# First rows as single transfers, two squares as operands by themselves, unread products beside the chain, and a bank cleared earlier, in a streaming encoder layer

## The chip, the cores and the metric

The kernel runs on one core of one Trainium2 chip. A core has TensorE (PE, the matrix products), VectorE (DVE), ScalarE (ACT), GpSimd (POOL) and SyncE (SP, here a queue that issues transfers); ACT also issues a few. Transfers run on 16 DMA engines. The metric is the device time of one execution in microseconds; a lower one is better. A change of less than 0.2% (about 4.5 us here) can hardly be told from none.

## The reference

One layer of a hybrid encoder over 2048 prompt tokens and 64 sample tokens, width 1024, in float32:

```
mod = silu(c) @ w_ada + b_ada          -> sh1, sc1, gt1, sh2, sc2, gt2
h   = rmsnorm(x, g1) * (1 + sc1) + sh1
u, q, k, v, o, gates = split(h @ w_in)
x   = x + gt1 * (concat(pool_mixer(u), mlstm(q, k, v, gates) * sigmoid(o)) @ w_out)
h2  = rmsnorm(x, g2) * (1 + sc2) + sh2
a, g = split(causal_conv3(h2 @ w_up) + b_conv)
x   = x + gt2 * ((silu(g) * a) @ w_down)
y   = rmsnorm(x, g_final)
```

rmsnorm(x, g) is x * rsqrt(mean(x*x) + 1e-6) * g. Beside y, the states of the pooling mixer, the matrix memory and the convolution are returned. Two places matter here: the first rmsnorm, with its modulation, of the first 512 tokens, and the last rmsnorm of the last 256 tokens.

## The kernel before, in words

Activations are kept with the 1024 features on partitions, as eight rows `x[k]` of 128 partitions, and tokens along the free dimension. Float32 products are made in three passes of a rounded format (`PASSES`): a weight or activation is split into a rounded part and a remainder. Small products stay in plain float32; each of these is two instructions on PE.

The attention part goes over four groups of 512 tokens (the last has the 64 samples besides), the feed-forward part over three groups of 704. In the last part of the last feed-forward group the down projection runs for two sections of columns, 0 to 448 and 448 to 704 (`ENDS`), so that the final norm of the first section runs beside the products of the second.

The order: SP's transfers and most of the attention part are placed by a planner, from estimated times and from the order in the text. Inside `tc.manual_schedule` the order on PE, ACT, DVE and POOL is that of the text; this holds for the first stage `first()` with the first V projection, and for the whole feed-forward part. Each engine works through its own queue in order.

Eight banks of 512 columns take PE's results: four of a pool `large` (`mm_ps()`), two of `small` and two of `third`; `m2_ps()` takes turns, two of `small` and then two of `third`.

The first stage. The first eight rows `x0` come as four transfers of two rows (L135, on SP's and ACT's queue by turns), then the small vectors `V` (L136). `first()` squares each row on ACT (L984), and DVE adds six of the squares into two accumulators (L989). Beside each row PE makes a product that nothing reads (L991, into `ptq`). `silu()` makes CA from V. `rstd_cols` (L485 to L493) sums the two accumulators over partitions by products with one column of ones, four blocks of tokens times two accumulators (L489), scales the sums on DVE and takes the power -0.5 on POOL. `mod_q(0)` makes the first quarter of the modulation: eight steps of four products with `CA` (L923), a copy by ACT (L930), a transposition (L932), and two additions on DVE into `MOD` (L936). Between its steps and its transposition stand four products (L1001) that spread the four columns of inverse roots over all partitions into `pr`. Then DVE scales the first rows by `pr` (L1005), PE makes two more unread products (L1010, into `psq`), `h0(0)` makes the normalised rows on ACT (L953), and the V projection starts (L1028).

The squares lie in the pool `scr` of five buffers. Two small operations that need `V` stand after the first stage in the text (L1420, L1421) and outside the written order.

The end. `down` makes a row's products (L1807), `down_end` adds them into the residual row on DVE (L1823), squares it on ACT and adds the square on POOL, except that the last row's square stays an operand of its own (L1833). `final_end` for the second section clears a bank on DVE (L1702), sums the squares over partitions (L1705), lets DVE work off some rows of the first section (`late[0]`, L1746), scales (L1661), takes the power on POOL (L1663), spreads the result twice (L1721), multiplies six rows on DVE (L1746) and two on POOL (L1759), and stores them (L1740).

Of the kernel before, what the change touches and what calls it, by code (L numbers as in the profile page):

```python
# [9 lines left out]
F32 = mybir.dt.float32  # L10
# [24 lines left out]
NH = 4  # L35
# [21 lines left out]
def tile_layer(ctx: ExitStack, tc: tile.TileContext, xT, vecs, cst, rst, w_mod, w_ada, w_qkou, w_v, w_pool,  # L57
# [75 lines left out]
    V = cp.tile([P, NV], F32, tag="V", name="V")  # L133
    for k in range(0, KD, 2):
        (act if k % 4 else nc.sync).dma_start(out=pair_of(x0[k:k + 2]), in_=xT[k:k + 2, :, 0:GT].rearrange("k p t -> p k t"))  # L135
    nc.sync.dma_start(out=V, in_=vecs)  # L136
# [675 lines left out]
    if True:  # L812
# [161 lines left out]
        def first():  # L974
# [4 lines left out]
            def silu():  # L979
                act.activation(CA.rearrange("p k s -> p s k"),  # L980
                               V[:, V_CP:V_CP + 16].rearrange("p (s k) -> p s k", s=2), AF.Silu)
            for k in range(KD):
                x, sq = x0[k], scr()
                act.activation(sq[:, :GT], x, AF.Square)  # L984
                if k < 2:
                    sums.append(sq)
                else:
                    acc = sums[k % 2]
                    dve.tensor_tensor(out=acc[:, :GT], in0=acc[:, :GT], in1=sq[:, :GT], op=ALU.add)  # L989

                pe.matmul(ptq[:, :256], x[:, :P], x[:, :256], start=True, stop=True)  # L991
            silu()
            rs = sm.tile([P, 5], F32, tag="rs", name="rs")
            rstd_cols(sums, o0, rs)
            mod = mod_q(0)
            for _ in range(KD + 1):
                next(mod)

            pr = third.tile([P, 512], F32, tag="bank", name="pr")
            for ti in range(4):  # L1000
                pe.matmul(pr[:, ti * P:(ti + 1) * P], rs[:, ti:ti + 1].broadcast_to([P, P]), ident, start=True, stop=True)  # L1001
            for _ in mod:
# [6 lines left out]
            for _ in range(2):  # L1009
                pe.matmul(psq[:, :256], x0[7][:, :P], x0[7][:, :256], start=True, stop=True)  # L1010
            us = h0(0)
# [392 lines left out]
        for o in groups:  # L1404
# [5 lines left out]
            if o.g == 0:  # L1410
                with tc.manual_schedule(engines={ET.PE, ET.Activation, ET.DVE, ET.Pool}):
                    ps_v = first()
                    small_inputs()
                    cols = []
                    va = proj_v(o, h, cols)
            else:
                cols = []
                va = proj_v(o, h, cols)
            if o.g == 0:
                dve.tensor_copy(M[:, GT + 1:GT + 2], RV[:, 2:3])  # L1420
                dve.tensor_scalar(out=GH, in0=V[:, V_GH:V_GH + NH], scalar1=0.5, scalar2=None, op0=ALU.mult)  # L1421
                t = scr()
# [264 lines left out]

    late, YLATE = [], 6

    def final_end(o, x3, sums, lo, hi):  # L1690
# [3 lines left out]
        for _ in range(4 if lo == 0 else 0):  # L1694
            yield
        ps = m2_ps()
        rs = f2.tile([P, 5], F32, tag="rs", name="rs", bufs=2)
        order = [(ti, i) for ti in range(len(tiles)) for i in range(len(sums))]
        if lo > 0:
            order.sort(key=lambda c: c[1])  # L1700
        if lo > 0:
            dve.memset(ps[:, :len(tiles)], 0.0)  # L1702
        for ti, i in order:
# [4 lines left out]
        if lo > 0:  # L1708
            late[0](YLATE)
        stat_cols(ps, rs, [n for (t, n) in tiles])  # L1710
        if lo > 0:
# [64 lines left out]
    for o in fgroups:  # L1776
        Bo = B[o.g]
        for pi, (f0, f1_) in enumerate(PARTS):
# [39 lines left out]
            def down_end(n, ps, secs):  # L1818
# [8 lines left out]
                lo, hi = secs[0][0], secs[-1][1]  # L1827
                if ends and n == KD - 1:
                    sq7 = fscr()
                    for (a, b, s) in o.segs:  # L1830
# [33 lines left out]
            for secs in [(c,) for c in ENDS] if ends else (both,):  # L1864
                sums = [(ssum, 0)]
                for n in range(NE, KD):
                    ps = [mm_ps() for _ in secs]
                    down(ps, rows[n], range(nf), secs, ends)
                    down_end(n, ps, secs)
# [89 lines left out]
```

## Time and profile before

| what | us |
|---|---|
| median of 3 runs | 2227.15 (2225.89 to 2227.29) |
| the profiled execution | 2230.81 |
| its span, first to last instruction | 2229.0 |
| PE busy, of the span | 2208.9 (99%) |
| DVE busy | 1572.2 (71%) |
| ACT busy | 1000.4 (45%) |

The 1.8 us between the profiled execution's time and its span lie around the span. A row of a timeline gives the start, the length, the engine, the line of the kernel, the operation, result and operands, the shape and how many instructions are merged; in brackets the idle time before it and what ended it. The windows give the busy time of each engine in a stretch, and the clock granted to PE as a share of full speed. Products are pipelined and their ends are modelled, so that starts are surer than lengths.

### The profile page before, as it was taken

How to read it: one execution, taken by the hardware profiler on the slowest of the kernel's cores; microseconds unless marked ns; L12 is line 12 of the kernel's file. 1: busy time of each engine (PE TensorE's matmuls, PEld its weight loads, DVE VectorE, ACT ScalarE, POOL GpSimd, SP SyncE). 2: the span in 40 equal slices, each digit the busy share in tenths (PEclk: the TensorE clock that was granted, in tenths of full speed). 3: DMA queues.
4: the chain of work that ended last, by engine and by line, in shares of the span. 5: the costliest groups of instructions: out<-in, count | busy, mean ns of one | idle time of the engine just before them, and what ended most of it. 6: DMA issues, size and time to landing. Idle time of an engine off the chain costs nothing.

```text
span 2229.0 us, 37990 instructions
## 1 busy us (share of the span) xinstructions
PE 2208.9 (99%) x13744; PEld 2102.7 (94%) x13744; DVE 1572.2 (71%) x2888; ACT 1000.4 (45%) x1981; POOL 192.5 (9%) x474
## 2 busy tenths in 40 slices
PE   8999999999999999999999999999999999999998
PEld 7888888888899999999999999999999999999998
DVE  5867668757955688687858587777766675757475
ACT  4644335234333455454536354545444343445254
POOL 0010000001000100010000210100001210101012
PEclk9999999999999999999999999999999999999999
DMA  9977997988879485747557775466458655353442
GB/s 350 330 251 228 300 305 254 306 286 266 296 253 299 148 269 164 243 163 270 179 176 243 263 263 176 156 213 198 143 160 290 196 167 167 111 171 116 145 148 81
DMA packets 284708, 487.26 MB, mean 219 GB/s; under 512 B 24640, under 2 KB 88512, under 8 KB 284520
## 3 DMA queue, kind: packets, MB, share of 16 engines
q1 hardware_dynamic: 275080, 462.52, 63.2%
q10 hardware_dynamic: 9440, 22.32, 2.6%
q8 instruction: 108, 1.77, 0.3%
q14 instruction: 80, 0.66, 0.1%
HBM read 378.68 MB, written 106.06 MB: 217 GB/s over the span
## 4 chain that ended last, share of the span: by engine, by line
PE 94%; DMA 3%; DVE 2%; issue 1%; SPq 0%; ACT 0%; POOL 0%; POOLq 0%; DVEq 0%; ACTq 0%
PE mm L1531 40%; PE mm L1807 23%; PE mm L445 23%; PE mm L1091 1%; DMA raw<-w_ada 1%; PE m L1280 1%; PE m L1300 1%; PE m L1302 1%; PE m L1265 1%; DMA wsum<-w 1%; PE mm L1028 1%; PE p L1028 1%; PE m L923 0%; PE m L1255 0%; DVE scr L237 0%
## 5 line engine op out<-in xcount | busy, mean ns | idle before, releaser
L1531 PE MATMUL mm<-hx,wt 128*128 128x352 f32 x5544 | 897.9, 323 | 1.9 <-ACT s L1570 1.3
L1531 PEld LDWEIGHTS mm<-hx,wt 128*128 128x128 f32 x5544 | 892.8, 188 | 2.6 <-ACT s L1570 1.6
L1807 PE MATMUL mm<-av,wt 128*128 128x352 f32 (+2 forms) x3168 | 514.5, 323 | 0.0
L1807 PEld LDWEIGHTS mm<-av,wt 128*128 128x128 f32 x3168 | 509.6, 188 | 1.2
L445 PE MATMUL mm<-hl,wt 128*128 128x512 f32 (+2 forms) x1920 | 389.7, 358 | 0.0
L379 ACT ACTIVATE wt<-raw 128x512 fp32r<-128x512 f32 (+3 forms) x518 | 286.2, 574 | 215.6 <-PE mm L445 77.6
L382 DVE TENSOR_TENSOR wt<-raw,wt 128x512 fp32r<-128x512 f32 (+3 forms) x518 | 324.4, 641 | 78.4 <-ACT wt L379 75.6
L445 PEld LDWEIGHTS mm<-hl,wt 128*128 128x128 f32 x1920 | 315.4, 189 | 52.5 <-issue 5.3
L1823 DVE SCALAR_TENSOR_TENSOR x<-mm,MOD,x 128x352 f32<-128x352 f32 (+4 forms) x224 | 106.5, 526 | 133.1 <-PE mm L1807 132.9
L445 PE MATMUL mm<-mx,wt 128*128 128x512 f32 (+1 forms) x960 | 185.3, 354 | 0.0
L445 PEld LDWEIGHTS mm<-mx,wt 128*128 128x128 f32 x960 | 159.1, 188 | 25.4
L1518 DVE SCALAR_TENSOR_TENSOR tg<-eg,V,tg 128x704 f32<-128x704 f32 (+1 forms) x132 | 125.7, 953 | 53.9 <-ACT tg L1513 51.6
L382 DVE TENSOR_TENSOR wt<-wt 128x512 fp32r<-128x512 f32 x176 | 121.7, 692 | 36.9 <-ACT wt L379 36.9
L1518 DVE SCALAR_TENSOR_TENSOR ta<-ea,V,ta 128x704 f32<-128x704 f32 (+1 forms) x132 | 125.7, 952 | 5.2 <-ACT ta L1513 2.6
L379 ACT ACTIVATE wt<-wt 128x512 fp32r<-128x512 f32 x176 | 108.3, 622 | 18.3 <-DMA wt<-wsum 14.6
L1579 ACT ACTIVATE u<-mm 128x352 f32<-128x352 f32 x66 | 30.7, 465 | 169.5 <-PE mm L1531 162.0
L1539 DVE TENSOR_TENSOR eg<-mm,u 128x352 f32<-128x352 f32 x154 | 70.2, 468 | 41.2 <-ACT u L1594 27.1
L1639 DVE TENSOR_TENSOR av<-tg,av 128x704 fp32r<-128x704 f32 (+1 forms) x88 | 60.6, 709 | 53.8 <-ACT av L1634 53.8
L1625 ACT ACTIVATE tg<-tg 128x704 f32<-128x704 f32 (+1 forms) x66 | 52.4, 794 | 78.5 <-DVE tg L1518 78.5
L1570 ACT ACTIVATE s<-mm 128x352 f32<-128x352 f32 x66 | 30.7, 465 | 111.4 <-PE mm L1531 106.9
L1091 PE MATMUL mm<-wt,hl 128*128 128x256 f32 (+1 forms) x576 | 70.7, 282 | 0.0
L1091 PEld LDWEIGHTS mm<-wt,hl 128*128 128x128 f32 x576 | 69.8, 188 | 0.9 <-issue 0.6
(293 smaller groups left out, 1954.3 us busy)
## 6 DMA issues: line engine op xcount, KB each, us to landing
raw<-w_up SPq DMA_DIRECT2D x198, 256.0 KB, 4.0
wt<-hl_kept SPq DMA_DIRECT2D x96, 512.0 KB, 6.0
wt<-wsum SPq DMA_DIRECT2D x176, 256.0 KB, 4.0
wt<-wsplit SPq DMA_DIRECT2D x88, 512.0 KB, 4.6
raw<-w_down SPq DMA_DIRECT2D x96, 256.0 KB, 3.0
w<-w_up SPq DMA_DIRECT2D x88, 256.0 KB, 4.0
wsum<-w SPq DMA_DIRECT2D x44, 512.0 KB, 5.1
wsplit<-wt SPq DMA_DIRECT2D x44, 512.0 KB, 3.3
```

The costliest lines, as they stand in the source:

```text
L379: act.activation(u.w[:, 0, :u.n], u.raw[:, :u.n], AF.Copy)
L382: dve.tensor_tensor(out=u.w[:, 1, :u.n], in0=u.raw[:, :u.n], in1=u.w[:, 0, :u.n].bitcast(F32), op=ALU.subtract)
L445: pe.matmul(ps[bi][:, :hi - lo], U[:, a, k % 4 * P:(k % 4 + 1) * P], mv[k][:, b, lo:hi], start=(at == 0 and pi == 0), stop=(k == order[-1] ...
L1028: pe.matmul(to[ti][:, :n], h[k][:, b, ti * P:(ti + 1) * P], w[:, a, k % 2 * n:(k % 2 + 1) * n], start=(hv == 1 and k == 0 and (a, b) == (0 ...
L1091: pe.matmul(ps[ti][:n, :cols], h[4 * kh + k4][:, b, lo:lo + n], U[:, a, k4 % 2 * cols:(k4 % 2 + 1) * cols], start=(kh == 0 and k4 == 0 and ...
L1518: dve.scalar_tensor_tensor(out=t[:, :E], in0=ext[:, j:j + E], scalar=wc(j, f), in1=t[:, :E], op0=ALU.mult, op1=ALU.add)
L1531: pe.matmul(ps[:, :FH], U[:, a, kc * P:(kc + 1) * P], Bo.at(nm, kc, b), start=(first and kc == 0 and pi == 0), stop=(kc == 3 and pi == 2), ...
L1539: dve.tensor_tensor(out=ext[:, d:d + b - a], in0=ps[:, a:b], in1=u[:, a:b], op=ALU.add)
L1625: act.activation(self.tg[:, :E], self.tg[:, :E], AF.Silu)
L1639: dve.tensor_tensor(out=self.d[:, 1, a:b], in0=self.tg[:, a + 2 * s:b + 2 * s], in1=self.d[:, 0, a:b].bitcast(F32), op=ALU.subtract)
L1807: pe.matmul(ps[i][:, :hi - lo], U[:, a, k % 4 * P:(k % 4 + 1) * P], av[k][:, b, lo:hi], start=(k == 0 and (a, b) == PASSES[0]), stop=(k == ...
L1823: dve.scalar_tensor_tensor(out=x3[n][:, a:b], in0=ps[i][:, a - lo:b - lo], scalar=gt2(n, s), in1=x3[n][:, a:b], op0=ALU.mult, op1=ALU.add)
```

## The change

Five pieces.

- The first eight rows come as eight transfers of one row, by turns on SP's and ACT's queue; V follows.
- In `first()` the squares of rows 6 and 7 are no longer added into the accumulators but are operands themselves: four additions on DVE instead of six, and sixteen one-column products instead of eight. They go into a bank `cols` of the pool `third`, cleared beforehand, square by square instead of block by block, and no longer through `rstd_cols` and its turn of `m2_ps()`.
- After each of the eight steps of `mod_q(0)` stands an unread product of 128 columns into `ptq`. The four products that spread the inverse roots become one of 512 columns: DVE multiplies the identity by the four columns (`dg`), and PE multiplies that by ones. The two unread products after it go into `ptq` instead of `psq`.
- The two small operations on V stand inside the written order, behind the first stage.
- At the end, the bank of the second section's sums is taken and cleared on DVE ahead of the last row's products; two unread products stand on PE ahead of the sums, and three behind them.

```diff
-    for k in range(0, KD, 2):
-        (act if k % 4 else nc.sync).dma_start(out=pair_of(x0[k:k + 2]), in_=xT[k:k + 2, :, 0:GT].rearrange("k p t -> p k t"))
+    for k in range(KD):
+        (act if k % 2 else nc.sync).dma_start(out=x0[k], in_=xT[k, :, 0:GT])
...
+            cols = third.tile([P, 512], F32, tag="bank", name="cols")
+            dve.memset(cols[:, :4], 0.0)
...
-                if k < 2:
+                if k < 2 or k > 5:
                     sums.append(sq)
...
             silu()
+            for sq in sums:
+                for ti in range(4):
+                    pe.matmul(cols[:, ti:ti + 1], sq[:, ti * P:(ti + 1) * P], ones[:, 0:1], start=False, stop=sq is sums[-1],
+                              skip_group_check=True)
             rs = sm.tile([P, 5], F32, tag="rs", name="rs")
-            rstd_cols(sums, o0, rs)
+            dve.tensor_scalar(out=rs[:, :4], in0=cols[:, :4], scalar1=1.0 / D, scalar2=EPS, op0=ALU.mult, op1=ALU.add)
+            pool.tensor_tensor(out=rs[:, :4], in0=rs[:, :4], in1=half[:, :4], op=ALU.pow)
             mod = mod_q(0)
-            for _ in range(KD + 1):
+            for k in range(KD):
                 next(mod)
+                pe.matmul(ptq[:, 256:384], x0[7][:, :P], x0[7][:, :P], start=True, stop=True)
+            next(mod)
+            dg = scr()
+            dve.tensor_tensor(out=dg[:, :GT].rearrange("p (t c) -> p t c", c=P),
+                              in0=ident.unsqueeze(1).broadcast_to([P, 4, P]),
+                              in1=rs[:, 0:4].unsqueeze(2).broadcast_to([P, 4, P]), op=ALU.mult)
             pr = third.tile([P, 512], F32, tag="bank", name="pr")
-            for ti in range(4):
-                pe.matmul(pr[:, ti * P:(ti + 1) * P], rs[:, ti:ti + 1].broadcast_to([P, P]), ident, start=True, stop=True)
+            pe.matmul(pr, ones, dg[:, :GT], start=True, stop=True)
...
-                pe.matmul(psq[:, :256], x0[7][:, :P], x0[7][:, :256], start=True, stop=True)
+                pe.matmul(ptq[:, 256:], x0[7][:, :P], x0[7][:, :256], start=True, stop=True)
...
                     ps_v = first()
+                    dve.tensor_copy(M[:, GT + 1:GT + 2], RV[:, 2:3])
+                    dve.tensor_scalar(out=GH, in0=V[:, V_GH:V_GH + NH], scalar1=0.5, scalar2=None, op0=ALU.mult)
                     small_inputs()
...
-    late, YLATE = [], 6
+    late, early, YLATE = [], [], 6
+
+    def busy(n):
+        for _ in range(n):
+            pe.matmul(early[1][:, :P], ident, ident, start=True, stop=True)
...
-        ps = m2_ps()
+        ps = m2_ps() if lo == 0 else early[0]
...
-        if lo > 0:
-            dve.memset(ps[:, :len(tiles)], 0.0)
...
         if lo > 0:
             late[0](YLATE)
+            busy(3)
...
                 if ends and n == KD - 1:
+                    if lo > 0:
+                        busy(2)
                     sq7 = fscr()
...
                     ps = [mm_ps() for _ in secs]
+                    if ends and n == KD - 1 and secs[0][0]:
+                        early.extend([m2_ps(), mm_ps()])
+                        dve.memset(early[0][:, :2], 0.0)
```

More of the change, by code (lines that the diff above doesn't have):

```diff
@@ L1419, in tile_layer @@
             if o.g == 0:
-                dve.tensor_copy(M[:, GT + 1:GT + 2], RV[:, 2:3])
-                dve.tensor_scalar(out=GH, in0=V[:, V_GH:V_GH + NH], scalar1=0.5, scalar2=None, op0=ALU.mult)
                 t = scr()
```

## The prediction

> **What bounds the kernel now.** I read the page first, then the waits of TensorE (PE), then the timelines of the two ends, which are the only places that the change touches, and last the granted clock in stretches of 3.41 us.
>
> The page gives the span, and the chain of work that ended last by engine:
>
> ```profile
> span 2229.0 us, 37990 instructions
> ...
> PE 94%; DMA 3%; DVE 2%; issue 1%; SPq 0%; ACT 0%; POOL 0%; POOLq 0%; DVEq 0%; ACTq 0%
> ```
>
> PE sets the time: what shortens PE's own sequence at the start moves everything behind it. Of the waits of PE, two lie in the attention part, where the order is planned and not written out:
>
> ```profile
> PE m L1255 <- DVE GL L237: 2.0, 1, 2.0
> PE m L1280 <- DVE kw L237: 2.0, 1, 2.0
> ```
>
> Timeline of PE at the start (start us, length, line, operation, tiles, shapes, count, idle before it and who ended it; a float32 product is two instructions). The last two rows are from the chain: the same 64 L923 instructions a quarter later, and the one-column products of the first final section:
>
> ```profile
> 5.67 6.16 PE L991 MATMUL m<-mx 128*128 128x256 f32 x16 [5.67 <-DMA mx<-xT]
> 12.72 0.35 PE L489 MATMUL m<-ones_r,scr 128*128 128x1 f32 x2 [0.89 <-DVE scr L989]
> 13.23 2.42 PE L489 MATMUL m<-ones_r,scr 128*128 128x1 f32 x14 [0.15 <-DVE scr L989]
> 15.58 3.59 PE L923 MATMUL m<-mx,CA 128*2 128x128 f32 x64
> 19.10 1.99 PE L1001 MATMUL pr<-V,rs 128*128 128x128 f32 x8
> 20.93 0.27 PE L932 MATMUL m<-V,scr 128*128 128x128 f32 x1
> 21.04 1.03 PE L1010 MATMUL m<-mx 128*128 128x256 f32 x4
> 22.69 2.88 PE L1028 MATMUL mm<-wt,hl 128*128 128x264 f32 x18 [0.62 <-ACT hl L953]
> ...
> 25.57 1.86 PE m L923 x64
> ...
> 2209.20 1.55 PE m L1705 x16
> ```
>
> From 5.67 on PE is nearly always busy, but slowly: L923 takes 3.52 us (15.58 to 19.10) and later 1.86. The windows say why (start:end, length, busy us and instructions of PE, PEld, DVE, ACT, POOL, granted clock, DMA share, GB/s):
>
> ```profile
> 3.82:7.23 3.41, 1.55 (x4) 1.29 (x5) 0.00 (x0) 1.58 (x4) 0.00 (x0) 1.00 1.05 399
> 7.23:10.64 3.41, 3.41 (x10) 2.69 (x9) 1.29 (x4) 1.68 (x4) 0.00 (x0) 1.00 1.05 386
> 10.64:14.06 3.42, 2.38 (x16) 1.84 (x14) 2.53 (x5) 1.50 (x4) 0.00 (x0) 1.00 1.05 387
> 14.06:17.47 3.41, 3.41 (x47) 2.80 (x50) 0.16 (x1) 0.00 (x0) 1.10 (x2) 0.50 1.05 390
> 17.47:20.88 3.41, 3.41 (x40) 2.65 (x33) 0.00 (x0) 0.81 (x2) 0.00 (x0) 0.50 1.06 387
> ...
> 263.23:266.64 3.41, 1.45 (x10) 1.00 (x9) 2.51 (x5) 0.19 (x1) 0.00 (x0) 1.00 0.80 267
> ...
> 2208.83:2212.24 3.41, 3.41 (x33) 3.38 (x32) 0.76 (x4) 0.63 (x2) 1.93 (x3) 1.00 0.00 0
> 2219.07:2222.48 3.41, 1.51 (x13) 1.31 (x12) 2.94 (x8) 1.02 (x3) 0.79 (x2) 1.00 0.68 260
> ```
>
> The clock is halved from 14.06 to 20.88. In the stretch ahead of the fall PE was busy 2.38 us, but half of that with one-column products; only some 1.2 us (35%) were wide ones. A stretch with 1.55 us of wide work starts nothing, and one of 1.45 us (263.23) is followed by half clock; 2208.83, with one-column products for 1.55 of its 3.41 us, is not. So I count wide products alone and put the border at about half a stretch.
>
> **The change, part by part.** The other engines at the start: ACT (three rows), DVE (three), POOL (one), then the wait of SP's queue and two transfers (the time to landing stands last; the first was issued at 1.33, the second at 5.6 to 5.7):
>
> ```profile
> 5.65 2.19 ACT L984 ACTIVATE scr<-mx 128x512 f32<-128x512 f32 x4 [2.89 <-DMA mx<-xT]
> 8.42 0.63 ACT L984 ACTIVATE scr<-mx 128x512 f32<-128x512 f32 x1 [0.58 <-DMA mx<-xT]
> 11.94 0.20 ACT L980 ACTIVATE CA<-V 128x16 f32<-128x16 f32 x1
> ```
> ```profile
> 9.35 0.14 DVE L1420 COPY M<-V 4x1 f32<-4x1 f32 x1 [7.95 <-DMA V<-vecs]
> ...
> 9.49 3.68 DVE L989 TENSOR_TENSOR scr<-scr 128x512 f32<-128x512 f32 x6
> ...
> 21.52 0.15 DVE L936 TENSOR_TENSOR MOD<-m,V 128x4 f32<-128x4 f32 x1
> ```
> ```profile
> 15.93 1.02 POOL L493 TENSOR_TENSOR rs<-rs,half 128x4 f32<-128x4 f32 x1 [13.02 <-DVE rs L491]
> ```
> ```profile
> SPq L909 <- DMA mx<-xT: 1.6, 1, 1.6
> ```
> ```profile
> mx<-xT ACTq DMA_DIRECT2D x1, 512.0 KB, 7.6
> ```
> ```profile
> mx<-w_mod SPq DMA_DIRECT2D x1, 512.0 KB, 9.1
> ```
>
> *Single transfers.* Pairs land at 5.65 and 8.42 on one queue, 2.8 us apart; a single row needs half, so the first lands at about 4.3 and the last still at 8.93 (1.33 + 7.6), the bytes being the same at 386 to 399 GB/s. SP waits at its ninth transfer for the first to land; eight rows now fill that, and V goes out at about 4.3. Its bytes stand behind the rows as before, so I keep its landing at 9.3 (0 to +1 us: CA, its first reader on the path, isn't needed before 12.9). The last of the first four w_mod pairs stays at 14.75 (5.65 + 9.1), ahead of its use.
>
> *M and GH later.* The additions start when squares are there, not at 9.49; four of 0.6 us instead of six are done by 9. DVE pays the two small operations (0.14 each) behind the first stage, where nothing waits.
>
> *Sixteen one-column products instead of eight.* From the tail's rows below, four such instructions take 0.44 us at full clock (2220.08 to 2220.52), 0.11 each. Thirty-two are 3.5 us, before 1.8. They must follow the eight unread L991 products, which need the last row: 8.93 + 0.43 = 9.4 if the clock is full by then. It is, if it rises at 7.23: the stretch from 3.82 then holds 2.9 us of L991 instead of 1.55. So the sums end at 12.9.
>
> *Eight unread products in the quarter.* Two instructions of 128 columns each; L1001 shows 0.23 at half clock (1.83 us over eight to the start of L932), so 0.11 at full: 0.22 per step beside 0.23 of L923 (1.86 over 8), 0.45 at full and 0.87 at half. Nothing covers them, they stand in PE's own queue: +1.8 to +3.5 us.
>
> *One product of 512 columns for pr.* 0.86 us at full clock against 0.9 for the four of L1001; the gain is the clock's. Its operand (DVE, about 0.6 us) follows POOL's 1.02 us behind the sums and is hidden by the quarter.
>
> On the trace's own clock stretches: sums until 12.9; then wide work for 1.15 of the stretch that ends at 14.06, 34% as before, so the clock falls again; 2.5 steps by 14.06, 3.9 at half clock by 17.47, the rest by 18.2; pr until 19.05. L932 stood at 20.93: -1.9 us. L1010 now writes the bank that L936 reads, and may start after 21.67 less the shift, not 21.04; the 0.62 that L1028 waits for ACT covers it (0 to +0.4, I take +0.2). That is -1.7. Where the stretches lie against the start of a run one profile can't say, and other places give up to -3.5 and +3.0 (below); I take **-1.0**.
>
> *Banks behind.* The sums no longer take a turn of the four small banks, so the second gate tile after the first stage shares a pool with the two whose copies ACT makes. The first one's wait there:
>
> ```profile
>   ACT va L237: 0.4, 1
> ```
>
> I take +0.3 (0 to +0.4). What the planner does with the attention part can't be seen; nearest rows are the two waits of 2.0 us: -4 if both go, +6 if three more come. I take 0, since PE waits there for nothing else.
>
> *The end.* PE's rows, then ACT's, DVE's and POOL's:
>
> ```profile
> 2220.08 0.58 PE L1705 MATMUL m<-ones_r,ssum 128*128 128x1 f32 x4 [0.86 <-DVE m L1702]
> 2220.52 0.58 PE L1705 MATMUL m<-ones_r,fscr 128*128 128x1 f32 x4
> 2222.14 1.79 PE L1721 MATMUL m<-V,rs 128*128 128x128 f32 x8 [1.04 <-POOL rs L1663]
> ```
> ```profile
> 2219.77 0.51 ACT L1833 ACTIVATE fscr<-x 128x192 f32<-128x192 f32 x2 [0.95 <-DVE x L1823]
> ```
> ```profile
> 2221.14 0.16 DVE L1661 TENSOR_SCALAR rs<-m 128x2 f32<-128x2 f32 x1 [0.17 <-PE m L1705]
> ```
> ```profile
> 2221.38 0.71 POOL L1663 TENSOR_TENSOR rs<-rs,half 128x2 f32<-128x2 f32 x1 [2.23 <-DVE rs L1661]
> 2224.49 1.41 POOL L1759 TENSOR_TENSOR y<-x,fscr 128x256 f32<-128x256 f32 x2 [2.41 <-ACT fscr L1727]
> ```
>
> With the bank cleared early the first four products run ahead of ACT's square, which ends at 2220.28 and is late next: the second four start at 2220.30, 0.2 us sooner. Two unread products (0.44 us) fit before, three (0.66) end at about 2221.4, ahead of POOL's result at 2221.9. They bring the stretch from 2219.07 to 1.85 us of wide work, 54%: if the clock holds, L1721's eight take 0.9 instead of 1.79. The stores behind share a busy queue (0.68 in that stretch), so I take **-0.6** (-1.1 to +0.3).
>
> Sum: -1.0 + 0.3 - 0.6 = -1.3 us. The profiled execution took 2230.81, 3.66 over the median of 2227.15; 2230.81 becomes 2229.5, and the median 2225.9.
>
> **A rule against the rows.** The Trainium skill (TensorE: Matmul & The Clock Gate, Part 1, the HAM clock gate) says that about 3.4 us of sustained activity frees the clock and about one idle window of that length throttles it. By that rule PE, which never idles long here, would keep full clock through the changed first stage, which is the first rival. The rows disagree: the longest gap before the fall at 14.06 is 0.89 us, and 14.06:17.47 is busy throughout at 0.50.
>
> **The rivals.**
> 1. *The clock never falls.* Sums to 12.9, eight steps of 0.45 to 16.5, pr to 17.4: -3.5 against 20.93; with the end at -1.1: -4.6, 2222.5. For it: the unread products lift the wide share. Against: the same 34% ahead of 14.06.
> 2. *Half clock from the one-column products on* (the slower side). If the clock rises only at 10.64, L991 ends at 10.9, and 32 instructions at 0.22 end at 17.9; 3.9 steps at half clock, 4.1 at full: 23.2, pr 24.0: +3.0 against 20.93. With +0.3 and -0.2: 2230.2. It decides from a clock at half when the sums begin.
> 3. *The planned part comes out in another order*, with three more waits of 2.0 us: 2231.9. For it: the sums' bank turn and DVE's order change. Against: no wait there is for a bank.
> 4. *It doesn't do what it says*: the last row still lands at 8.93, and the doubled products eat what the rest brings; 2227.2.
>
> **How the numbers follow.** Forecast 0.42 (its own range 2223 to 2229), rivals 0.24, 0.12, 0.14, 0.08. The bound of 0.2% is 4.5 us, about what a measurement tells from no change: under 2222.7 or over 2231.6. Faster: most of rival 1 and the low end of the forecast, 0.22; slower: most of rival 3 and rival 2 with one more wait, 0.16; within: 0.62. The range 2221.5 to 2231.5 reaches from rival 1 to just below 3.
>
> **What would show it.** Right: first L991 near 4.3, additions before 9, the first L1028 near 21, a half-clock stretch from about 14, L1705's wait on the clearing gone, its second four 0.2 us sooner. Wrong: L1028 under 19.5 (rival 1) or over 23 (2), or new waits of PE between 55 and 640 us (3).

## The result, and the profile after

The changed kernel takes 2233.18 us (median, 2230.89 to 2235.85), the kernel before on the same chip 2227.22 (2224.85 to 2230.37). The ratio is 1.0026, with a 95% interval of 1.0016 to 1.0036: slower by 3.6 to 8.0 us. The forecast was 2225.9 and its range ended at 2231.5; the time lies above both. The profiled execution took 2234.15 us with a span of 2232.3, 3.3 us over that of before (whose profiled execution, 2230.81, was above all its timed ones).

PE is still 99% busy, with 5.8 us more of busy time than before, and no new wait of PE is longer than the 0.5 us for MOD at L1023 (the 0.6 for ACT at L1028 is gone for it). So no wait took the place of one that was removed; PE had more to do, and did part of it more slowly. The waits (total us, times, longest):

```profile
PE m L994 <- DMA mx<-xT: 4.7, 1, 4.7
...
PE m L1293 <- DVE kw L237: 0.4, 1, 0.4
...
PE m L1721 <- ACT fscr L1852: 0.2, 1, 0.2
```

L994, L1293 and L1721 were L991, L1280 and L1705 before; the longest other wait, for GL, went from 2.0 to 2.7. PE's timeline at the start (L998 are the sums, L1007 the new unread products, L1014 is `pr`, L1041 the first product of the V projection):

```profile
4.69 5.57 PE L994 MATMUL m<-mx 128*128 128x256 f32 x16 [4.69 <-DMA mx<-xT]
10.09 3.63 PE L998 MATMUL cols<-ones_r,scr 128*128 128x1 f32 x32
13.65 0.40 PE L923 MATMUL m<-mx,CA 128*2 128x128 f32 x8
13.98 0.49 PE L1007 MATMUL m<-mx 128*128 128x128 f32 x2
14.40 0.40 PE L923 MATMUL m<-mx,CA 128*2 128x128 f32 x8
...
16.33 0.61 PE L923 MATMUL m<-mx,CA 128*2 128x128 f32 x8
...
17.59 0.60 PE L923 MATMUL m<-mx,CA 128*2 128x128 f32 x8
...
22.50 1.91 PE L1014 MATMUL pr<-scr,ones_r 128*128 128x512 f32 x2
24.20 0.42 PE L932 MATMUL m<-V,scr 128*128 128x128 f32 x1
25.14 2.08 PE L1023 MATMUL m<-mx 128*128 128x256 f32 x4 [0.52 <-DVE MOD L936]
26.66 3.57 PE L1041 MATMUL mm<-wt,hl 128*128 128x264 f32 x18
```

The V projection starts at 26.66 instead of 22.69, although PE's first product starts 0.98 us sooner (4.69 against 5.67). A step of the quarter with its unread product takes 0.75 us (13.65 to 14.40) and then 1.26 (16.33 to 17.59), eight of them 8.85 us (13.65 to 22.50). The windows show what happens at 15.29 (start:end, length, busy us and instructions of PE, PEld, DVE, ACT, POOL, granted clock, DMA share, GB/s):

```profile
8.46:11.87 3.41, 3.41 (x26) 3.21 (x24) 0.69 (x2) 1.26 (x3) 0.00 (x0) 1.00 1.00 357
11.87:15.29 3.41, 3.41 (x45) 2.68 (x44) 0.40 (x2) 0.00 (x0) 1.10 (x2) 1.00 1.05 396
15.29:18.70 3.41, 3.41 (x30) 1.72 (x22) 0.45 (x1) 0.00 (x0) 0.00 (x0) 0.50 1.06 388
18.70:22.11 3.41, 3.41 (x31) 1.53 (x30) 0.00 (x0) 0.07 (x1) 0.00 (x0) 0.50 1.05 392
22.11:25.52 3.41, 2.89 (x6) 1.33 (x7) 0.83 (x5) 0.81 (x3) 0.00 (x0) 0.50 1.05 405
25.52:28.94 3.41, 3.41 (x13) 3.06 (x13) 3.35 (x7) 3.26 (x6) 0.00 (x0) 0.50 1.00 374
28.94:32.35 3.41, 3.41 (x77) 2.99 (x76) 2.16 (x5) 0.00 (x0) 0.00 (x0) 1.00 0.82 281
```

The clock is halved for four stretches, 15.29 to 28.94; before it was two. PE was busy for the whole of the stretch ahead of the fall, but with one-column products until 13.65. The engines that were to be sooner are sooner (DVE's last additions, POOL's power, each one view of its own):

```profile
7.85 1.29 DVE L992 TENSOR_TENSOR scr<-scr 128x512 f32<-128x512 f32 x2 [0.19 <-ACT scr L986]
```
```profile
14.00 1.02 POOL L1002 TENSOR_TENSOR rs<-rs,half 128x4 f32<-128x4 f32 x1 [9.72 <-DVE rs L1001]
```

To see where the loss goes afterwards I use one landmark in all traces: the start of the long run of L445 products at about 56 us, behind the first L1134 and L1135. Before and after:

```profile
56.17 14.13 PE L445 MATMUL mm<-hl,wt 128*128 128x512 f32 x60
```
```profile
60.71 9.51 PE L445 MATMUL mm<-hl,wt 128*128 128x512 f32 x40
```

It is 4.54 us late there. The medians differ by 6.0 us (5.2 when the changed kernel ran again, below); where the rest lies, one pair of profiles does not show. The unchanged first stage itself moves from one execution to the next: it was traced in three more kernels below, and the first product of the V projection starts there at 22.81, 22.91 and 21.21 instead of 22.69. So a difference of 1.5 us between two traces at this place may come from the executions alone. In this pair of profiles part of it vanishes at 270 us, but for a reason on the side of before: that execution had one more halved stretch, 266.64 to 270.06 (the stretch of 1.45 us busy that the prediction quoted stands right ahead of it), and a wait of 2.0 us (L1280) that is 0.4 us after.

The end: PE, ACT and POOL.

```profile
2223.14 0.61 PE L1721 MATMUL m<-ones_r,fscr 128*128 128x1 f32 x4 [0.18 <-ACT fscr L1852]
...
2224.78 1.16 PE L1738 MATMUL m<-V,rs 128*128 128x128 f32 x8 [0.27 <-POOL rs L1676]
```
```profile
2222.72 0.51 ACT L1852 ACTIVATE fscr<-x 128x192 f32<-128x192 f32 x2 [0.96 <-DVE x L1840]
```
```profile
2226.50 1.41 POOL L1776 TENSOR_TENSOR y<-x,fscr 128x256 f32<-128x256 f32 x2 [1.77 <-ACT fscr L1744]
```

From ACT's last squares to POOL's `y` the chain takes 3.78 us (2222.72 to 2226.50) instead of 4.72 (2219.77 to 2224.49): 0.94 us less, as intended.

### The profile page after: what moved, and what is told of

The parts are those of the page before. It is cut to its first block, busy times and chain, and to the rows that moved or that the text cites. A ratio compares the mean times of both kernels' runs of the same rounds, so it can differ in the third digit from the quotient of the medians.

```text
span 2232.3 us, 38070 instructions
## 1 busy us (share of the span) xinstructions
PE 2214.7 (99%) x13780; PEld 2105.5 (94%) x13780; DVE 1570.7 (70%) x2888; ACT 999.2 (45%) x1981; POOL 193.7 (9%) x474
## 3 DMA queue, kind: packets, MB, share of 16 engines
q8 instruction: 109, 1.79, 0.3%
## 4 chain that ended last, share of the span: by engine, by line
PE 93%; DMA 4%; DVE 2%; issue 1%; ACT 0%; SPq 0%; POOL 0%; POOLq 0%; DVEq 0%; ACTq 0%
PE mm L1544 40%; PE mm L1824 23%; PE mm L445 22%; DMA raw<-w_ada 2%; PE mm L1104 1%; DMA wsum<-w 1%; PE m L1293 1%; PE m L1315 1%; PE m L1313 1%; PE m L1278 1%; PE mm L1041 1%; PE p L1041 1%; PE m L923 0%; DVE scr L237 0%; DMA w<-w_up 0%
## 5 line engine op out<-in xcount | busy, mean ns | idle before, releaser
L445 PE MATMUL mm<-hl,wt 128*128 128x512 f32 (+2 forms) x1920 | 388.6, 358 | 0.0
L445 PEld LDWEIGHTS mm<-hl,wt 128*128 128x128 f32 x1920 | 314.6, 188 | 52.2 <-issue 5.3
L445 PE MATMUL mm<-mx,wt 128*128 128x512 f32 (+1 forms) x960 | 185.3, 354 | 0.0
L445 PEld LDWEIGHTS mm<-mx,wt 128*128 128x128 f32 x960 | 159.1, 188 | 25.4
```

What stands on the lines that cost most here:

```text
L445: pe.matmul(ps[bi][:, :hi - lo], U[:, a, k % 4 * P:(k % 4 + 1) * P], mv[k][:, b, lo:hi], start=(at == 0 and pi == 0), stop=(k == order[-1] ...
```

## The experiments

The questions were which piece loses the time, whether the clock is the mechanism, why no gain of the start ever reaches the end, and what the end is worth. The theories, with the letters that the expectations use: the unread products alone bring the loss (A), *a reordered middle* does, by the bank turn or the planner (B), or *the doubled sums alone* (C). After the first four runs (without the unread products, six additions, the end, the rows) came *the clock and the combination* (A2: sixteen more one-column instructions leave too little wide work in a stretch, the clock falls, and the unread products then run at half clock and, being narrow, don't bring it back), and against it *the two pieces cost their own time and the costs add* (D) and *the unread products cost the same wherever they stand*. For the third question, *transfers set the pace up to about 55 us* (T). Ratios below are to the kernel before on the same chip, with 95% intervals.

**Without the unread products.**

```diff
             for k in range(KD):
                 next(mod)
-                pe.matmul(ptq[:, 256:384], x0[7][:, :P], x0[7][:, :P], start=True, stop=True)
```

> The changed kernel without the eight unread products in the first quarter of the modulation. Theory A (these products cost their own time and hold the clock at half while they last; they take 5.2 us in the trace of the changed kernel): the first L1041 some 5 us sooner than 26.7, the time about 2228. Theory B (the turn of the banks or the planned part of the attention brings the loss): the head gets shorter but the time stays within 1 us of 2233, with new waits of PE between 55 and 640 us. Theory C (sixteen one-column products instead of eight bring the loss): under 2 us gained, about 2231.5.

Measured: 1.0006 (0.9997 to 1.0015). The loss is gone, but there is no gain, although the start is 4.2 us faster than before, 8.2 us faster than in the changed kernel. Theory A had forecast 5 us and theory C under 2; both were too low, and B's loss did not stay. PE's timeline:

```profile
9.84 3.63 PE L998 MATMUL cols<-ones_r,scr 128*128 128x1 f32 x32
13.40 1.49 PE L923 MATMUL m<-mx,CA 128*2 128x128 f32 x48
...
18.51 2.90 PE L1040 MATMUL mm<-wt,hl 128*128 128x264 f32 x18
...
54.47 0.27 PE L1146 MATMUL m<-V,gt 128*4 128x128 f32 x1 [3.03 <-ACT va L237]
...
55.70 14.55 PE L445 MATMUL mm<-hl,wt 128*128 128x512 f32 x55
```

The clock did not fall: in the stretch 11.43 to 14.84 the sums stop at 13.40 and the rest, 42%, is wide. At 54.47 a wait of 3.03 us eats most of the gain, and the stretch that it empties is followed by a halved one:

```profile
52.39:55.80 3.41, 1.06 (x9) 0.73 (x10) 2.00 (x4) 2.88 (x7) 0.00 (x0) 1.00 1.02 381
55.80:59.22 3.41, 3.41 (x11) 2.64 (x10) 3.41 (x7) 2.59 (x3) 0.00 (x0) 0.50 1.05 389
```

**Six additions again, with the unread products** (eight one-column products, sixteen instructions), and **neither piece**.

```diff
-                if k < 2 or k > 5:
+                if k < 2:
```

> The changed kernel with six additions and eight one-column products (16 instructions) again, the unread products kept. Theory A: the one-column products save 1.8 us at full clock, the steps of 0.75 to 1.26 us stay: about 2231, head 2 us shorter. Theory C: most of the loss goes, 2228 or less, and the half-clock stretch gets shorter than 13.7 us. Theory B: no change, 2233.

> The changed kernel without the unread products in the quarter and with six additions again; single rows, written order, one product for pr and the end are kept. Fourth corner beside the changed kernel (both), the one without unread products, and the one with six additions. Theory A2 (neither piece is dear alone: thirty-two one-column instructions let the clock fall, and the unread products then run at half clock and are too narrow to raise it): 2226 to 2228, like the other two corners, and 5 to 7 us under the changed kernel. Theory D (the two pieces each cost their own time, and the costs add): some 2 us below each of the other corners, 2225 or less.

Measured: 0.9996 (0.9987 to 1.0005) with the unread products, 1.0003 (0.9994 to 1.0011) with neither. In both the clock stays full through the start. Six additions with the unread products came out as theory C had it (2228 or less); A had said 2231. Since leaving out the unread products alone also removes the loss, neither A nor C fits both runs. With the unread products the first product of the V projection starts at 20.49, 2.0 us later than with neither (18.46). Their own cost is more than that: a step takes 0.75 us, 0.33 of it up to the unread product (11.98 to 12.31), so each adds 0.42, 3.4 us in all. With neither, the quarter waits twice for its weights, 1.5 us together, and these waits are gone with the unread products. First the kernel with the unread products, then the one with neither:

```profile
11.98 0.40 PE L923 MATMUL m<-mx,CA 128*2 128x128 f32 x8
12.31 0.49 PE L1007 MATMUL m<-mx 128*128 128x128 f32 x2
12.73 0.40 PE L923 MATMUL m<-mx,CA 128*2 128x128 f32 x8
...
20.49 2.87 PE L1041 MATMUL mm<-wt,hl 128*128 128x264 f32 x18
```
```profile
13.84 0.62 PE L923 MATMUL m<-mx,CA 128*2 128x128 f32 x16 [0.73 <-DMA mx<-w_mod]
15.20 0.62 PE L923 MATMUL m<-mx,CA 128*2 128x128 f32 x16 [0.74 <-DMA mx<-w_mod]
```

**The changed kernel again**, beside the others.

> The changed kernel once more, beside the others on one chip. Theory A2: a half-clock stretch of 10 us or more in the quarter again, first L1041 at 24 to 27, the ratio to before 1.002 to 1.003. If that stretch is an accident of one profile: a stretch of 7 us or less, and the ratio still at 1.002 for another cause.

Measured: 1.0021 (1.0011 to 1.0032). The half clock lasts three stretches here (12.96 to 23.20), the first product starts at 26.97. So the four combinations of the two pieces are, with everything else of the change in all of them:

| squares and unread products | ratio | first product of V, us | landmark (56.17 before), us |
|---|---|---|---|
| neither | 1.0003 (0.9994 to 1.0011) | 18.46 | 54.55 |
| squares as operands only | 1.0006 (0.9997 to 1.0015) | 18.51 | 55.70, then a halved stretch |
| unread products only | 0.9996 (0.9987 to 1.0005) | 20.49 | 55.25 |
| both (the change), two runs | 1.0026 and 1.0021 | 26.66 and 26.97 | 60.71 and 61.05 |

At the first product the squares show no cost alone (0.05 us), the unread products 2.0 us, and both together 8.2 us. It is an interaction, and the clock is the larger part of it, but not all. An estimate from the rows says how much: at full clock throughout, the changed kernel's steps would end at 19.65 (13.65 and eight times 0.75), and with the 2.62 us that the kernel with six additions takes from there to the V projection (17.87 to 20.49) this would start at 22.3. So of the 8.2 us some 4.4 are the clock, and 3.8 are the two pieces' own time. Alone, each piece hid part of its own time in the waits for weights, 1.5 us with neither and 0.4 with the squares as operands. A reordered middle is out: the rows that follow the same text and bank turn, without one of the two pieces, lose nothing.

**The unread products among the sums.** The direct test: the same number and form of PE's instructions, eight of them in another place.

```diff
                 for ti in range(4):
                     pe.matmul(cols[:, ti:ti + 1], sq[:, ti * P:(ti + 1) * P], ones[:, 0:1], start=False, stop=sq is sums[-1],
                               skip_group_check=True)
+                    if ti % 2:
+                        pe.matmul(ptq[:, 256:384], x0[7][:, :P], x0[7][:, :P], start=True, stop=True)
...
                 next(mod)
-                pe.matmul(ptq[:, 256:384], x0[7][:, :P], x0[7][:, :P], start=True, stop=True)
```

> The changed kernel with its eight unread products moved: one after every second pair of one-column instructions' product within the sums, none between the steps of the modulation quarter. The number and the form of PE's instructions are those of the changed kernel; only their place differs. Theory A2 (the 32 one-column instructions in a row leave too little wide work in a stretch of 3.41 us, the clock falls, and the unread products behind them run at half): the sums are mixed with wide work, the clock stays full, sums from 10.1 to about 17 us, steps of 0.33 us, first product of the V projection near 22 us (18.5 without the unread products plus eight times 0.42), some 4.5 us sooner than in the changed kernel; ratio 0.999 to 1.0005. Rival (the unread products cost the same wherever they stand, and the clock is not what matters): the first product of the V projection stays at 26 to 27 us, ratio 1.002 to 1.003. Rival within A2 (128 columns are too few to count against the one-column ones): the clock falls in the sums, they take 7 to 9 us, first product at 24 to 27 us.

Measured: 0.9999 (0.9990 to 1.0008). PE's timeline (L1001 are the unread products here, L1042 is the V projection), and the windows:

```profile
15.22 0.78 PE L1001 MATMUL m<-mx 128*128 128x128 f32 x2
15.93 3.18 PE L923 MATMUL m<-mx,CA 128*2 128x128 f32 x64
...
21.76 2.90 PE L1042 MATMUL mm<-wt,hl 128*128 128x264 f32 x18
```
```profile
11.73:15.15 3.41, 3.41 (x33) 3.41 (x32) 0.00 (x0) 0.00 (x0) 0.00 (x0) 1.00 1.05 396
15.15:18.56 3.41, 3.41 (x56) 2.40 (x59) 0.85 (x2) 0.00 (x0) 1.10 (x2) 0.50 1.05 385
18.56:21.97 3.41, 2.89 (x28) 1.55 (x21) 1.62 (x7) 1.67 (x4) 0.00 (x0) 1.00 1.06 390
```

The landmark is at 56.78. 21.76 was forecast at 22, but the reason given failed: the clock did fall, at 15.15. It stayed at half for a single stretch, which from 15.93 on holds nothing but L923 in a row, and nearly all the unread products had been done at full clock before. So the place of the unread products decides 4.9 us (26.66 to 21.76). By an estimate from the rows, the half clock costs 1.65 us here (L923 3.11 us instead of 1.86, the last unread product 0.71 instead of 0.31) and 4.4 in the changed kernel: 2.7 of the 4.9 us are the clock. The other 2.2 are own time at full clock, since a group of four one-column instructions and an unread product takes 0.67 us here (10.13 to 10.80), where the same four take 0.45 in a row (3.56 over eight) and the product 0.42 between the steps; and the steps behind it come to 1.86 us in a row instead of 2.64 (eight times 0.33). "They cost the same wherever they stand" is out.

**Wider unread products**, 256 columns instead of 128.

```diff
-                pe.matmul(ptq[:, 256:384], x0[7][:, :P], x0[7][:, :P], start=True, stop=True)
+                pe.matmul(ptq[:, 256:], x0[7][:, :P], x0[7][:, :256], start=True, stop=True)
```

> The changed kernel with unread products of 256 columns instead of 128 in the quarter. Theory A2 (their share of wide work decides how long the half clock lasts): the half-clock stretch at the start ends after one or two stretches of 3.41 us instead of four, the first L1041 at 23 to 25 instead of 26.7, the time 1 to 3 us below the changed kernel. Theory D (their own time): each step 0.1 to 0.2 us longer, the time 1 to 2 us above the changed kernel.

Measured: 1.0018 (1.0010 to 1.0027), first product at 27.57. The half clock lasts two stretches (13.04 to 19.86) instead of three or four, but a step takes 1.69 us at half clock and 0.96 at full:

```profile
15.50 0.61 PE L923 MATMUL m<-mx,CA 128*2 128x128 f32 x8
16.04 1.22 PE L1007 MATMUL m<-mx 128*128 128x256 f32 x2
17.19 0.61 PE L923 MATMUL m<-mx,CA 128*2 128x128 f32 x8
...
20.25 0.40 PE L923 MATMUL m<-mx,CA 128*2 128x128 f32 x8
...
21.21 0.40 PE L923 MATMUL m<-mx,CA 128*2 128x128 f32 x8
```

Denser work brings the clock back sooner, as theory A2 has it, but its forecast of the gain failed (first product at 23 to 25, 1 to 3 us under the changed kernel): the wider products pay it all in their own time. D's forecast of 1 to 2 us above the changed kernel did not come either.

**The two remaining pieces alone**: the end, and the single rows with the two small operations moved.

```diff
-        ps = m2_ps()
+        ps = m2_ps() if lo == 0 else early[0]
...
+            busy(3)
...
+                    if lo > 0:
+                        busy(2)
```

> The kernel before with the change at the end alone. Theories A and C: 0.4 to 0.9 us faster than before (the last products L1721 at full clock, the sums 0.2 us sooner), the head as before. If the stores set the end: no change within 0.3 us. Theory B says nothing of it.

```diff
-    for k in range(0, KD, 2):
-        (act if k % 4 else nc.sync).dma_start(out=pair_of(x0[k:k + 2]), in_=xT[k:k + 2, :, 0:GT].rearrange("k p t -> p k t"))
+    for k in range(KD):
+        (act if k % 2 else nc.sync).dma_start(out=x0[k], in_=xT[k, :, 0:GT])
...
                     ps_v = first()
+                    dve.tensor_copy(M[:, GT + 1:GT + 2], RV[:, 2:3])
+                    dve.tensor_scalar(out=GH, in0=V[:, V_GH:V_GH + NH], scalar1=0.5, scalar2=None, op0=ALU.mult)
```

> The kernel before with single first rows and the two small operations inside the written order, nothing else. Theory A and C: the additions end 2 us or more sooner, the first products of the projection start 1.5 to 3 us sooner than 22.69 unless the clock falls longer, 2224 to 2226. If the last row's landing alone sets the start: within 1 us of before.

Measured: 1.0000 (0.9992 to 1.0009) for the end, 0.9998 (0.9989 to 1.0007) for the rows. The end does what was read from it (the eight L1725 products take 1.16 us instead of 1.79, POOL's `y` starts 3.78 us behind ACT's last squares, as in the changed kernel), and it is too small to measure (0.4 to 0.9 us were expected, and the interval reaches 2 us to either side):

```profile
2223.08 1.16 PE L1725 MATMUL m<-V,rs 128*128 128x128 f32 x8 [0.26 <-POOL rs L1663]
```

With the rows alone the first L1028 starts 2.47 us sooner, at 20.22, and at the landmark 1.67 us are left (54.50 against 56.17). The start came out as expected, the time (2224 to 2226 expected) did not: 2227.41. The quarter waits for its weights twice:

```profile
14.13 0.82 PE L923 MATMUL m<-mx,CA 128*2 128x128 f32 x16 [0.72 <-DMA mx<-w_mod]
15.49 1.03 PE L923 MATMUL m<-mx,CA 128*2 128x128 f32 x16 [0.53 <-DMA mx<-w_mod]
...
20.22 2.96 PE L1028 MATMUL mm<-wt,hl 128*128 128x264 f32 x18
```

**Why the gains don't arrive: fewer bytes.** The kernel without unread products, and the kernel before, each without the transfers of the second quarter's weights (2.1 MB), so that this quarter of the modulation holds its bias alone:

```diff
-                        pin(nc.sync.dma_start(out=c_q[qn][i], in_=w_mod[qn, i]))
+                        pool.memset(c_q[qn][i], 0.0)
```

> The changed kernel without the unread products, and with the eight transfers of the second quarter of the modulation's weights (2.1 MB) left out: their tiles are set to zero by POOL instead, so this quarter of the modulation holds only its bias. Theory T (the transfers set the pace until about 55 us, and there a start 4 us sooner is given back by waits of ACT for weights): PE's waits for ACT at 55 us go, and a start 4 us sooner is still there at 60 us. If the wait has to do with ACT's or PE's order: it stays, and the gain is gone at 60 us as without this edit.

> The kernel before, with the eight transfers of the second modulation quarter (2.1 MB) left out and that quarter's weights set to zero on GpSimd, so the quarter is only its bias: part of the computation is left out. Theory T (up to about 55 us the transfers set the pace, and eat what the first stage gains): the kernel before is itself not held up by transfers there, its first L1028 stays near 22.7, and it gains little from the missing bytes: ratio 0.998 to 1.000 against the kernel before, the waits of ScalarE for w_v, w_qkou and w_pool between 20 and 60 us shrink, and PE's starts behind 60 us move by less than 1.5 us. Rival (the missing work itself is worth the 4 us, whatever the first stage does): 4 us here as well, ratio near 0.998.

Measured: 0.9991 (0.9982 to 0.9999) for the first, 0.9996 (0.9987 to 1.0005) for the kernel before. These intervals overlap; the traces are clearer. In the first, ACT's waits between 18 and 60 us are down to 1.6 us from 12.6 (without unread products, full loads: w_v 7.7, w_qkou 2.5, w_pool 2.4), the wait for `va` is gone, and the whole gain of the start, 4.4 us (18.31 against 22.69), is still there at the landmark (51.70 against 56.17):

```profile
51.70 14.83 PE L445 MATMUL mm<-hl,wt 128*128 128x512 f32 x63
```

The kernel before gains nothing from the same missing bytes (landmark 56.32):

```profile
56.32 13.90 PE L445 MATMUL mm<-hl,wt 128*128 128x512 f32 x59
```

So the transfers set the pace up to 55 us only for a kernel that starts faster. With all loads, gains of 4.2 us at the first product are down to 0.5 and 1.6 at the landmark (without the unread products, and with neither piece), and those of 2.2 and 2.5 us to 0.9 and 1.7; the loss of the change stays. Whether it is the bytes or the place of these transfers in the queue was not separated. And the landmark is not the end: of the 4.4 us only 2.0 (0.2 to 4.0) are there in the time, and what became of the rest is not shown.

**Later loads.** The loads of the second group's eight rows behind the first head's projections, on the kernel with neither piece, and on the kernel before.

```diff
-                    nc.sync.dma_start(out=xs[-1], in_=xT[k + i, :, o.t0:o.t0 + o.T])
+                    if o.g != 1:
+                        nc.sync.dma_start(out=xs[-1], in_=xT[k + i, :, o.t0:o.t0 + o.T])
...
+                    if o.g == 0:
+                        for k, x in enumerate(xs):
+                            nc.sync.dma_start(out=x, in_=xT[k, :, GT:2 * GT])
```

> The changed kernel with six additions and without the unread products (first product of the V projection at 18.5 us, clock never halved at the start), and the loads of the eight rows of the second group of 512 tokens (2.1 MB) issued after the first head's projections instead of early. Nothing is left out. Theory T: ScalarE then gets w_v, w_qkou and w_pool sooner, PE's wait for va near 55 us goes from 2.1 to under 0.5 us, and some 4 us of the start's gain stay behind 60 us: ratio 0.998 (2223 to 2226 us). Rival (the rows of the second group become late themselves, or the planner's order changes): a new wait of PE or ScalarE for x behind 60 us, ratio 0.9995 to 1.003.

> The kernel before with the same later loads alone. Theory T: no gain, since the kernel before does not wait there: ratio 0.9993 to 1.0007, first L1028-like product still near 22.7. Rival (the later loads are worth something by themselves, or cost): a shift of PE behind 60 us of 2 us or more to either side.

Measured: 1.0004 (0.9995 to 1.0013) and 0.9998 (0.9989 to 1.0007). The first expectation failed. ACT's wait for w_v is still 5.6 us and that for w_pool 2.4; PE's waits for `va` are shared out (1.1, 0.3 and 0.3) but the landmark is at 54.83, no better than the 54.55 without the edit. These rows were not the main thing in the way of w_v (its wait was 7.1 without the edit). On the kernel before, the ratio came out as expected, but the first product did not stay near 22.7:

```profile
21.21 2.87 PE L1029 MATMUL mm<-wt,hl 128*128 128x264 f32 x18 [0.62 <-ACT hl L954]
```

Here the clock was halved for one stretch (15.82 to 19.24) instead of two, and the 1.5 us are still there at the landmark (54.60). Nothing in the first stage was edited, so this is most likely where the stretches lay in this execution. Which order of the loads would keep the gain stays open. No version that leaves nothing out was measurably better than the kernel before; the best, with 0.9996, has an interval that holds 1.

## Why the prediction was wrong

**Single transfers, M and GH, the additions: right; the quarter's weights: too early.** First product at 4.69 (about 4.3 was forecast), V's transfer at 4.84, the additions done at 9.14. The sums began at 10.09 instead of 9.4, since the clock rose at 8.46 in this execution and not at 7.23: L994's instructions start 0.43 us apart up to 8.26 and 0.22 apart from 8.58. (The column of the granted clock reads 1.00 ahead of its first change too; the distances show that it was half.) That put the end of the sums at 13.65 instead of 12.9: +0.75 us. The weights of the quarter were put too early: 14.75, "ahead of its use". In the faster starts PE waits for the last of them until 15.20 (neither piece) and 15.25 (squares as operands); the changed kernel shows no such wait, as its seventh step, the first to need them, starts at 20.11.

**The fall of the clock: right.** It came at the end of the stretch that the sums half fill, at 15.29 on this execution's grid. The reading behind it, that one-column products don't count, held at the start of all traces; the border of half a stretch was put too high (last section).

**"Eight unread products in the quarter": the step that failed.** I priced the step at 0.45 us at full clock and 0.87 at half, by adding 0.22 of unread product to 0.23 of L923. It took 0.75 and 1.26. The 0.23 were read from L923 in a row and the 0.11 per unread instruction from L1001 in a row; alternating between the two shapes costs 0.30 us a step at full clock that neither row shows (the kernel with six additions has the same 0.75 at full clock throughout). What in the alternation costs it was not separated. The text then let the clock rise after one stretch, at 17.47, with the same mixture running; it stayed at half for four stretches here and three in the repeat. The steps took 8.85 us instead of 5.3 (12.9 to 18.2): +3.55. `pr` behind them, still at half clock, took 1.70 instead of 0.85, and from L932 to the V projection 2.46 instead of 1.96: +0.85 and +0.50. Together 5.65 us, which is all of the distance from the forecast 20.99 (22.69 - 1.7) to 26.66. With the measured prices and a clock that rises at 18.70, the steps would have ended at 21.0 instead of 22.50, by an estimate from these rows: so some 2.1 of the 3.55 us are the price of the alternation, and 1.5, with the 0.85 and the 0.50, are the clock that stayed at half.

**The rivals.** Rival 2, half clock from the sums on, named the half clock as the loss, but its condition (the clock at half when the sums begin) was not met: the sums began at full clock (in the repeat they lost it half way, at 12.96), and most of the loss came behind them. Its mark, a first product later than 23, was passed, but by another way. Its price, +3.0 us, counted the same steps too cheaply and a quick rise; 4.0 to 4.3 us were measured at the first product, 4.5 at the landmark. Rival 1, a clock that never falls at the start, happens when either of the two pieces is left out, but even then its 3.5 us don't reach the end.

**"What shortens PE's own sequence at the start moves everything behind it": wrong.** It held for the loss of the change. Of gains of 4 us at the start 0.5 to 1.6 us were left at the landmark. PE's 94% of the chain and its short list of waits are those of a kernel whose loads are just in time; 4 us sooner, ACT waits for w_v, w_qkou and w_pool, and PE for ACT. The DMA column of the windows, 386 to 399 GB/s at the start, stood in the quoted rows, and I used it for the first rows only.

**Banks behind, and the planned part: right, at about nothing.** No wait for a bank showed, the 0.52 at L1023 is for MOD, and is covered by the one that L1028 had before (at full clock, without the unread products, L932 to the V projection takes 1.75 us, before 1.76), and the planned part has no new wait over 0.3 us (that for GL went from 2.0 to 2.7, one for kw from 2.0 to 0.4).

**The end: right on the chain, without effect that can be measured.** 0.94 us were gained from ACT's square to POOL's `y` (0.6 was forecast, up to 1.1), L1738 took 1.16 instead of 1.79, the second four sums wait 0.18 for ACT. In the profiled pair the span behind POOL's `y` is 1.3 us longer (2232.3 - 2226.50 against 2229.0 - 2224.49), so that the gain was gone behind it, where the stores are; alone on the kernel before it measured 1.0000. What the stores wait for was not separated.

**The rule against the rows.** The Trainium skill (TensorE: Matmul & The Clock Gate, Part 1, the HAM clock gate) lets an idle window throttle the clock and sustained activity free it. The runs disagree on both sides: the fall at 15.29 follows a stretch in which PE was busy for 3.41 of 3.41 us, and 18.70 to 22.11, as busy, did not end the half clock.

## What to carry to other kernels

Price filler on PE by rows in which the two shapes alternate, and by how much wide work it adds to a stretch; here a narrow filler between the steps cost 0.42 us at full clock and 0.72 at half, where a row of its own shape shows 0.22, and it hardly brought the clock back. The same eight among the one-column products put the V projection off by 3.3 us (18.51 to 21.76) instead of 8.2. Two pieces that are each harmless can lose time together, through the clock and because a wait hides the cost of each alone, so test them in all four combinations. Before counting a gain at the start, look whether the next stage's loads would be there sooner as well: here, with transfers at 390 GB/s from the start, they weren't. And trace an unchanged stage more than once before reading 1.5 us out of it.

## What was not expected of the hardware

- At the start, whether the clock falls goes by wide work. Counted from start to start, with the alternating products at their durations in a row (0.45 of the 0.75 us of a step), the full-clock stretches that were followed by half clock held 24% to 42% of wide work (42% is the 1.45 us at 263.23 before), those of the start that were followed by full clock 41% and more (42% without the unread products). So the border is near two fifths, not a half; it is an estimate from the starts. Further in, two stretches lie above it. With no one-column products in them, PE was busy for 1.49 of 3.41 us (44%) from 262.67 on in the changed kernel with later loads, and for 1.90 (56%) from 641.02 on in the repeat of the changed kernel, and half clock followed both times. So busy wide time alone is not the whole rule.
- The way back needs more. A stretch filled by L923 in a row (nearly filled, where the unread products stand among the sums), with the L1001 of before behind it or not, ended the half clock each time, and so did the first whole stretch of the 256-column mixture. The 128-column mixture (0.87 of 1.26 us by the rows in a row, 69%) fills two whole stretches in each of two executions: it ended the half clock in one of these four (19.79 to 23.20 of the repeat) and not in the others.
- Halved stretches turn up far from the start too, where the grid of 3.41 us happens to cut a short wait: at 55.80 without the unread products, at 266.64 in the profile of before, at 644.43 in the changed kernel's repeat. Where the grid lies against the start differs between executions (the clock fell at 15.29 and at 12.96 in two executions of the changed kernel). That may be part of the 5 to 10 us between the shortest and the longest execution of one kernel; it was not separated.
